# Four 128-column turns a head, from TensorE to VectorE blocks and two transfers, in a decoder step with a gated delta rule

## The chip, the cores and the metric

The kernel runs on one core of one Trainium2 chip. The metric is the device time of one execution in microseconds (us), from its first to its last instruction with what the chip adds around it; a time is given as the median of several runs. A profile is one further execution, recorded instruction by instruction; its span is the time between the first and the last recorded instruction.

The engines are named as in the profile: PE is TensorE (PEld its weight loads), DVE is VectorE, ACT is ScalarE, POOL is GpSimd, and SP is SyncE, which here only issues DMAs. Each engine works through its own list in order. An engine that waits for something holds up everything behind it in its list.

## The reference

One inference step of a one-layer decoder: 512 prompt tokens and 8 sample tokens, model width 2048, in float32. The first half of the layer mixes tokens by two groups, a gated delta network of 8 heads of dimension 128 and a multi-scale pool; the second half is a gated feed-forward network of width 5632. What the change touches is the delta network of the prompt. Cut to that, with `c` a chunk of tokens:

```python
q, k = l2norm(q) * HEAD_DIM ** -0.5, l2norm(k)          # per head, over its 128 channels
gc = cumsum(g); decay = tril(exp(gc[:, None] - gc[None, :]))
m = strict_tril((k * beta) @ k.T * decay)               # (I + m) is inverted
u = solve(I + m, v * beta); w = solve(I + m, k * beta * exp(gc))
qk = tril(q @ k.T * decay)
for each chunk:                                         # S is the 128 x 128 state
    v_new = u - w @ S
    o = (q * exp(gc)) @ S + qk @ v_new
    S = S * exp(g_last) + (k * exp(g_last - gc)).T @ v_new
dn_out = rmsnorm(o, dn_norm) * silu(z)
```

`q`, `k`, `v` come from one input projection, a causal convolution over 4 tokens and silu. `dn_out` and the pool's output go through an output projection, are added to the input, and the feed-forward part follows.

## The kernel before, in words

Nearly all of the work is matrix products in three passes: each operand is cut into a high and a low float32r part (ScalarE copies the high part, VectorE subtracts for the low one), and high x high, high x low and low x high are summed (L168 to L170 in the first half, L1222 to L1224 in the second). Weights stream in as pieces of 512 KB ("raw", three buffers), issued by SyncE (L131); ScalarE (L135) and VectorE (L137) cut each piece, with a priority ahead of all other work.

The first half runs over tiles of 128 output columns: `product` does 16 steps of 6 passes into two accumulators of 264 and 256 columns. The order of the tiles is: keys of heads 0 to 3, the output gate z of heads 0 to 3, queries and values of heads 0 to 3, the same for heads 4 to 7, then the pool's tiles. The first two key tiles belong to the start of the kernel. Activations are held with channels on the 128 partitions and tokens along them; `qkv_tile` (L730) makes the convolution and silu of one tile in this form.

The small work of the delta network is woven in between the steps of the products. A `Weave` (L43) holds tasks that are Python generators: after each step of a product it lets a task go on to its next `yield n`, which asks to be called again n steps later. TensorE's order is exactly the order in which the program is written. The other engines' orders in this part are made by a planner that takes an instruction when its inputs are expected and follows the priorities. In the second half all orders are as written.

The tasks, with 128 tokens (a chunk) at a time, four chunks to a head:

- `gates` makes the decay exponents once, and writes them to DRAM (`gcr_d`, L621).
- `keys(h)` (L760): `decay(h)` (L743) fetches the head's decay row for all partitions (`gcb`) and makes the decay matrix `dm`; the product of the keys with themselves goes to `gp_` (L766); the keys are turned to tokens on partitions by four TensorE transposes (L769) into `ktp`. ScalarE sums squares of `ktp`, GpSimd takes the root (`pow_mhalf`, L215: `rr`), VectorE scales `gp_` to `nn` (L781) and the turned keys to `kd` (L783). Four DMAs (L788) then store the 32x32 diagonal blocks of `nn` in DRAM (`nd_d`), and GpSimd zeroes them (L791).
- `eliminate(b)` (L794), for four heads at once: the blocks come back as `nb` (L797), 31 steps of two VectorE operations (L807, L809) invert them into `u`, and the inverse and its transpose go to DRAM (`ud_d`, L810, L813).
- `qv_tiles(h)` (L1089) fetches the inverse into `utf` by four DMAs (L1093), makes the query tile, then the value tile, and adds `delta`.
- `delta(h)` (L817) makes the decay again; multiplies `nn` with the inverse (L831); turns the queries (L838) for the sums of their squares and the root `fq`; refines the inverse in three steps (`for it`, L846: products L850, correction L852 into `cur`, named `uu` in the trace), with the query-key product (L857) and `aq` (L860) in step 0 and the turn of the values (L865) and their scaling to `vs` (L867) in step 1. Then the recurrence runs over the four chunks: `R` (L879), `W` (L884, L886), the state `S` (L889, L894) and the output in `op_` (L895, L896). At the end the output is normed into `on`, in the place of `nn`.
- `gate(h)` (L913) turns `on` back by four transposes (L916) and multiplies it into the silu of z (L918).

The transposes write to PSUM, so ScalarE and VectorE read the turned form there.

Of the kernel before, what the change touches and what calls it, by code (L numbers as in the profile page):

```python
# [17 lines left out]
P = 128  # L18
D = 2048
KT = D // P  # L20
NB = 8
SEQ = 512
NTOK = NB + SEQ
H = 8
# [12 lines left out]
    "qts": 1, "fq": 2, "aq": 1, "vs": 1, "R": 2, "W": 2, "S": 2, "so": 2, "ro": 2, "s0": 2, "s2": 1, "kd": 4, "st": 2,  # L37
# [32 lines left out]
def decoder_kernel(ctx, tc, x_prompt, x_sample, state_delta, state_conv, state_pool, norm_mix, w_in,  # L70
# [450 lines left out]
    with ExitStack() as p1:  # L521
# [29 lines left out]
        def gates():  # L551
# [69 lines left out]
            sp.dma_start(gcr_d, gr)  # L621
# [120 lines left out]

        def decay(h):  # L743
# [16 lines left out]
        def keys(h):  # L760
            kT, nn = mixb[:, h % 4, 0:SEQ], mixb[:, 4 + h % 4, 0:SEQ]
            kd = kds[h] = d1tile("kd", [P, SEQ], "kd")
# [4 lines left out]
            ktp = pst()  # L767
            for c in range(NCH):
                te.transpose(ktp[:, ck(c)], kT[:, ck(c)], ident)  # L769
            ss = d1tile("ss", [P, NCH], "ss")  # L770
            squares(ktp, ss)
# [11 lines left out]
            dve.tensor_tensor(v3(kd), v3(ktp), bc3(ad), op=ALU.mult)  # L783
            yield 6 if h < 3 else 2
            nn3 = v3(nn)
            for q in range(4):
                r = slice(32 * q, 32 * q + 32)
                sp.dma_start(nd_d[h, q].rearrange("c s j -> s c j"), nn3[r, :, r])  # L788
# [5 lines left out]
        def eliminate(b):  # L794
            hs = slice(4 * b, 4 * b + 4)
            nb = d1tile("nb", [64, 32, 32], "nb")
            sp.dma_start(nb.rearrange("p s j -> p (s j)"), nd_d[hs].rearrange("h q c s j -> (h q c) (s j)"))  # L797
# [12 lines left out]
            sp.dma_start(ud_d[hs, :, 0].rearrange("h q c s j -> (h q) c (s j)"), uf)  # L810
            ut = d1tile("nb", [64, 32, 32], "ut")
            dve.tensor_copy(ut, u.rearrange("p s j -> p j s"))
            sp.dma_start(ud_d[hs, :, 1].rearrange("h q c s j -> (h q) c (s j)"), ut.rearrange("p s j -> p (s j)"))  # L813
# [3 lines left out]
        def delta(h, qT, vT):  # L817
# [18 lines left out]
            qtp = pst()  # L836
            for c in range(NCH):
                te.transpose(qtp[:, ck(c)], qT[:, ck(c)], ident)  # L838
            ss = d1tile("ss", [P, NCH], "ss")
            squares(qtp, ss)  # L840
            dve.tensor_scalar(ss, ss, EPS, None, op0=ALU.add)
            fq = d1tile("fq", [P, NCH], "fq")
            pow_mhalf(fq, ss)
            dve.tensor_scalar(fq, fq, float(P) ** -0.5, None, op0=ALU.mult)
            yield 2
            for it in range(3):  # L846
# [7 lines left out]
                if it == 0:  # L854
                    gq_ = pst()
# [6 lines left out]
                if it == 1:  # L862
                    vtp = pst()
                    for c in range(NCH):
                        te.transpose(vtp[:, ck(c)], vT[:, ck(c)], ident)  # L865
                    vs = d1tile("vs", [P, SEQ], "vs")
                    dve.tensor_tensor(v3(vs), v3(vtp), bc3(ik), op=ALU.mult)  # L867
# [4 lines left out]
            for c in range(NCH):  # L872
                if S is None:
                    R = vs[:, ck(c)]
                else:
# [3 lines left out]
                    dve.scalar_tensor_tensor(Rt, kp[:, 0:P], negc[:, c, h:h + 1], vs[:, ck(c)],  # L879
                                             op0=ALU.mult, op1=ALU.add)  # L880
# [17 lines left out]
                yield 1  # L898
            sp.dma_start(nd_prompt[0, 0, h], S)
# [11 lines left out]
            weave.add(gate(h, on), 1, 8)  # L911

        def gate(h, on):  # L913
            otp = pst()
            for c in range(NCH):
                te.transpose(otp[:, ck(c)], on[:, ck(c)], ident)  # L916
            yield 1
            dve.scalar_tensor_tensor(mix[h][:, NB:NTOK], otp, dnw, mix[h][:, NB:NTOK], op0=ALU.mult, op1=ALU.mult)  # L918
# [170 lines left out]
        def qv_tiles(h):  # L1089
            utf = utfs[h % 2].rearrange("p a c j -> p (a c) j")  # L1090
            for q in range(4):
                r = slice(32 * q, 32 * q + 32)
                sp.dma_start(utf[r, :, r], ud_d[h, q].rearrange("a c s j -> s (a c) j"))  # L1093
            qT = d1tile("s0", [P, SEQ], "qT")
            qkv_tile(0, h, qT)
            vT = d1tile("s2", [P, SEQ], "vT")
            qkv_tile(2, h, vT)
            weave.add(delta(h, qT, vT), 0, 1)

        kds = {}  # L1100
        for b in range(2):
            for h in range(4 * b, 4 * b + 4):
                qkv_tile(1, h, mixb[:, h % 4, 0:SEQ],
                         {0: ext_first, 1: ext_second}.get(h))
                if h == 0:
                    weave.add(states())
                    weave.add(gates(), 1)
# [969 lines left out]
```

## Time and profile before

| | us |
|---|---|
| runs | 2160.15, 2160.83, 2162.0 |
| median of the runs | 2160.83 |
| profiled execution: span | 2158.9 |
| PE busy | 2136.1 (99%) |
| DVE busy | 1746.4 (81%) |
| ACT busy | 929.6 (43%) |
| POOL busy | 433.8 (20%) |
| granted TensorE clock | 0.999 |

Of the profiled execution the span is all that is recorded; the runs' times have a little more around it. The first half of the layer lasts until about 615 us, and the work that the change touches lies between about 75 and 520 us.

How to read the rows: an instruction is named by its line in the kernel, its engine, its operation, and the tiles out<-in by the program's names. "x8" counts instructions. In groups, the two numbers behind the shapes are busy us and mean ns of one; what follows is the idle time of the engine just before them and what ended it. In a view of waits, "A <- B: 2.4, 3, 1.1" says that A waited for B for 2.4 us in total, 3 times, at most 1.1 us. In a timeline the first column is the start in us, the second the duration of the (merged) row. TensorE's instructions overlap in its pipeline, so the distance between two starts, not the duration, is what one costs.

### The profile page before, as it was taken

How to read it: one execution, taken by the hardware profiler on the slowest of the kernel's cores; microseconds unless marked ns; L12 is line 12 of the kernel's file. 1: busy time of each engine (PE TensorE's matmuls, PEld its weight loads, DVE VectorE, ACT ScalarE, POOL GpSimd, SP SyncE). 2: the span in 40 equal slices, each digit the busy share in tenths (PEclk: the TensorE clock that was granted, in tenths of full speed). 3: DMA queues.
4: the chain of work that ended last, by engine and by line, in shares of the span. 5: the costliest groups of instructions: out<-in, count | busy, mean ns of one | idle time of the engine just before them, and what ended most of it. 6: DMA issues, size and time to landing. Idle time of an engine off the chain costs nothing.

```text
span 2158.9 us, 42980 instructions
## 1 busy us (share of the span) xinstructions
PE 2136.1 (99%) x17809; PEld 2128.8 (99%) x17809; DVE 1746.4 (81%) x2619; ACT 929.6 (43%) x1404; POOL 433.8 (20%) x512
## 2 busy tenths in 40 slices
PE   8999999999999999999999999999999999999998
PEld 7999999999999999999999999999999999999998
DVE  7786667666499979988988888888877898887997
ACT  6533443432264545434433434434334444435444
POOL 2210110111012202233233233232113302003100
PEclk9999999999999999999999999999999999999999
DMA  8343234323445543554554454454446746438343
GB/s 281 92 110 91 76 94 112 88 76 96 120 121 161 152 119 111 155 166 141 145 166 139 147 167 143 142 163 134 125 147 189 234 111 205 115 103 247 93 108 119
DMA packets 442497, 297.04 MB, mean 138 GB/s; under 512 B 26556, under 2 KB 423253, under 8 KB 438957
## 3 DMA queue, kind: packets, MB, share of 16 engines
q1 hardware_dynamic: 422733, 219.94, 36.3%
q0 software_dynamic: 18256, 73.55, 10.5%
q8 instruction: 139, 2.28, 0.5%
q10 hardware_dynamic: 1312, 0.80, 0.1%
q14 instruction: 57, 0.47, 0.1%
HBM read 251.47 MB, written 43.43 MB: 137 GB/s over the span
## 4 chain that ended last, share of the span: by engine, by line
PE 86%; DVE 8%; DMA 2%; issue 2%; ACT 1%; POOL 1%; SPq 0%; DVEq 0%; POOLq 0%; ACTq 0%
PE dn L1223 20%; PE dn L1222 20%; PE dn L1224 20%; PE mm L168 6%; PE mm L170 6%; PE mm L169 6%; DVE lo L1216 2%; DVE raw L1244 1%; PE dn L850 1%; DMA st<-a_d 1%; DVE lo L137 1%; POOL st L1776 0%; DMA xt<-in_x_prompt_dram 0%; PE dn L960 0%; PE dn L857 0%
## 5 line engine op out<-in xcount | busy, mean ns | idle before, releaser
L1215 ACT CAST hi<-raw 128x1024 fp32r<-128x1024 f32 (+1 forms) x422 | 427.4, 1027 | 400.2 <-DVE raw L1244 206.5
L1216 DVE TENSOR_TENSOR lo<-raw,hi 128x1024 fp32r<-128x1024 f32 (+1 forms) x422 | 527.4, 1270 | 87.1 <-ACT hi L1215 85.6
L168 PE MATMUL mm<-xh,hi 128*128 128x256 f32 (+1 forms) x1280 | 379.7, 297 | 2.4 <-DVE mixa L259 2.4
L169 PE MATMUL mm<-xl,hi 128*128 128x256 f32 (+1 forms) x1280 | 361.5, 282 | 0.9 <-DVE xl L350 0.7
L170 PE MATMUL mm<-xh,lo 128*128 128x256 f32 (+1 forms) x1280 | 361.8, 283 | 0.4 <-DVE lo L137 0.4
L168 PEld LDWEIGHTS mm<-xh,hi 128*128 128x128 f32 x1280 | 241.4, 189 | 3.7 <-DVE mixa L259 3.1
L169 PEld LDWEIGHTS mm<-xl,hi 128*128 128x128 f32 x1280 | 241.7, 189 | 1.7 <-DVE xl L350 1.7
L170 PEld LDWEIGHTS mm<-xh,lo 128*128 128x128 f32 x1280 | 240.8, 188 | 0.6 <-DVE lo L137 0.6
L1244 DVE TENSOR_TENSOR raw<-raw 128x1024 f32<-128x1024 f32 (+1 forms) x130 | 175.3, 1349 | 2.2
L1223 PE MATMUL dn<-b21l,hi 128*128 128x260 f32 x620 | 175.7, 283 | 0.4 <-DVE b21l L1786 0.4
L1224 PE MATMUL dn<-b21h,lo 128*128 128x260 f32 x620 | 175.4, 283 | 0.0
L1222 PE MATMUL dn<-b21h,hi 128*128 128x260 f32 x620 | 175.0, 282 | 0.0
L1224 PE MATMUL dn<-b11h,lo 128*128 128x260 f32 x612 | 173.4, 283 | 1.2 <-DVE lo L1216 1.1
L1223 PE MATMUL dn<-b11l,hi 128*128 128x260 f32 x612 | 173.3, 283 | 0.0
L1222 PE MATMUL dn<-b11h,hi 128*128 128x260 f32 x612 | 172.7, 282 | 0.0
L1222 PE MATMUL dn<-T1h,hi 128*128 128x260 f32 x556 | 158.1, 284 | 0.0
L1223 PE MATMUL dn<-T1l,hi 128*128 128x260 f32 x556 | 157.7, 284 | 0.0
L1224 PE MATMUL dn<-T1h,lo 128*128 128x260 f32 x556 | 156.7, 282 | 0.0
L1222 PE MATMUL dn<-B22h,hi 128*128 128x260 f32 x548 | 155.9, 284 | 0.0
L1223 PE MATMUL dn<-B22l,hi 128*128 128x260 f32 x548 | 155.6, 284 | 0.0
L1224 PE MATMUL dn<-B22h,lo 128*128 128x260 f32 x548 | 154.6, 282 | 0.4 <-DVE lo L1216 0.4
L135 ACT CAST hi<-raw 128x1024 fp32r<-128x1024 f32 (+2 forms) x86 | 87.1, 1014 | 148.2 <-PE mm L169 139.4
(659 smaller groups left out, 6422.5 us busy)
## 6 DMA issues: line engine op xcount, KB each, us to landing
raw<-in_w_gate_up_dram SPq DMA_DIRECT2D x134, 512.0 KB
raw<-in_w_in_dram SPq DMA_DIRECT2D x79, 512.0 KB
a_d<-mixa POOLq DMA_DIRECT2D x22, 1040.0 KB, 5.5
raw<-in_w_down_dram SPq DMA_DIRECT2D x48, 448.0 KB
mixb<-in_w_gate_up_dram SPq DMA_DIRECT2D x41, 512.0 KB
raw<-in_w_out_dram SPq DMA_DIRECT2D x25, 512.0 KB
st<-a_d POOLq DMA_DIRECT2D x49, 260.0 KB, 6.5
raw<-in_w_down_dram SPq DMA_DIRECT2D x24, 512.0 KB
```

The lines of the kernel that those rows point to most:

```text
L135: act.copy(hi[:, r], raw[:, r])
L137: dve.tensor_tensor(lo[:, r], raw[:, r], hi[:, r].bitcast(F32), op=ALU.subtract)
L168: te.matmul(acc[ci], wh, hi[k][:, c0:c1], start=(k == 0), stop=False)
L169: te.matmul(acc[ci], wh, lo[k][:, c0:c1], start=False, stop=False)
L170: te.matmul(acc[ci], wl, hi[k][:, c0:c1], start=False, stop=(k == len(w) - 1))
L850: te.matmul(yp[0:96, c, j], xt_[:, c, :], udf[:, c, j] if it == 0 else v3(cur)[:, c, j], start=True, stop=True)
L1215: act.copy(hi, raw)
L1216: dve.tensor_tensor(lo, raw, hi.bitcast(F32), op=ALU.subtract)
L1222: te.matmul(acc, wh[:, k, :], xf[:, k, :], start=start and k == 0, stop=False)
L1223: te.matmul(acc, wh[:, k, :], xg[:, k, :], start=False, stop=False)
L1224: te.matmul(acc, wl[:, k, :], xf[:, k, :], start=False, stop=stop and k == wh.shape[1] - 1)
L1244: dve.tensor_tensor(r[name], r[a], r[b], op=op)
```

## The change

Each of the four turns of a head leaves TensorE. `turn_blocks(kind, h, src, dst)` lets VectorE transpose the 32x32 blocks of a 128x512 tile in place in their grid (`bt`), SyncE writes the result to a DRAM tile `tok_d`, and four more DMAs read it back in another order, so that the blocks change places as well. Kinds 1 (keys) and 3 (normed output) are read in pieces of 128 bytes; for kinds 0 (queries) and 2 (values) VectorE writes the blocks so that the pieces have 512 bytes, and the turned tile has its columns in another order, which the views `by_chunk` and `by_column` undo.

With that, the order of several steps changes. The key tile is turned as soon as it is made, into `kd`, and scaled later, in step 0 of the refinement. The squared norms of the keys are the diagonal of `gp_`, read by VectorE with the unit matrix. The value tile is made and turned before the query tile. The query-key product and `aq` go from step 0 to step 2 of the refinement. The turned queries are only used for their norms, by ScalarE after the second chunk. The output is turned at the end of `delta`, and `gate` comes 12 steps later instead of 8.

The DMAs of the decay rows (`gcr_d`, `gcb`), of the diagonal blocks (`nd_d`, `nb`) and of the inverse (`ud_d`, `utf`) are issued by GpSimd instead of SyncE. The descriptor scratch is 8192 instead of its default, and the tiles `vs`, `bt` and `tq` get 2, 2 and 1 buffers of 128x512.

```diff
-            sp.dma_start(gcr_d, gr)
+            pool.dma_start(gcr_d, gr)
...
+        tok_d = dram.tile([4, H, P, SEQ], F32, name="tok_d")
+        def by_chunk(a):
+            return a.rearrange("p (i c q) -> p c i q", i=4, c=NCH)
+        def by_column(a):
+            return a.rearrange("p (i q) -> p i q", i=4)
...
+        def turn_blocks(kind, h, src, dst):
+            bt, d = d1tile("bt", [P, SEQ], "bt"), tok_d[kind, h]
+            if kind % 2:
+                dve.transpose(bt, src)
+                d = d.rearrange("p f -> (p f)").rearrange("(c p f) -> c p f", c=NCH, p=P)
+                sp.dma_start(d.rearrange("c p f -> p c f"), v3(bt))
+                rows = d.rearrange("c (i p) (j q) -> j p (c i) q", p=32, q=32)
+            else:
+                dve.transpose(bt.rearrange("p (j c q) -> p c j q", j=4, c=NCH),
+                              src.rearrange("p (c j q) -> p c j q", j=4, c=NCH))
+                sp.dma_start(d, bt)
+                rows = d.rearrange("(i p) (j f) -> j p i f", p=32, j=4)
+            for j in range(4):
+                sp.dma_start(dst[32 * j:32 * j + 32, :].rearrange("p (n q) -> p n q", n=rows.shape[2]), rows[j])
...
-            sp.dma_start(gcb, gcr_d[h:h + 1, :].broadcast_to([P, SEQ]))
+            pool.dma_start(gcb, gcr_d[h:h + 1, :].broadcast_to([P, SEQ]))
...
-            ktp = pst()
+            ss = d1tile("ss", [P, NCH], "ss")
+            junk = d1tile("junk", [P, P], "junk")
             for c in range(NCH):
-                te.transpose(ktp[:, ck(c)], kT[:, ck(c)], ident)
-            ss = d1tile("ss", [P, NCH], "ss")
-            squares(ktp, ss)
+                dve.scalar_tensor_tensor(junk, gp_[:, ck(c)], 1.0, ident, op0=ALU.mult, op1=ALU.mult,
+                                         accum_out=ss[:, c:c + 1])
...
-            dve.tensor_tensor(v3(kd), v3(ktp), bc3(ad), op=ALU.mult)
...
-                sp.dma_start(nd_d[h, q].rearrange("c s j -> s c j"), nn3[r, :, r])
+                pool.dma_start(nd_d[h, q].rearrange("c s j -> s c j"), nn3[r, :, r])
...
-            qtp = pst()
-            for c in range(NCH):
-                te.transpose(qtp[:, ck(c)], qT[:, ck(c)], ident)
...
                 if it == 0:
+                    dve.tensor_tensor(v3(kd), v3(kd), bc3(sck[:, h, 2, :]), op=ALU.mult)
+                if it == 2:
                     gq_ = pst()
...
                 if it == 1:
-                    vtp = pst()
-                    for c in range(NCH):
-                        te.transpose(vtp[:, ck(c)], vT[:, ck(c)], ident)
-                    vs = d1tile("vs", [P, SEQ], "vs")
-                    dve.tensor_tensor(v3(vs), v3(vtp), bc3(ik), op=ALU.mult)
+                    scaled(vs, ik)
...
-            weave.add(gate(h, on), 1, 8)
+            turn_blocks(3, h, on, on)
+            weave.add(gate(h, on), 1, 12)
         def gate(h, on):
-            otp = pst()
-            for c in range(NCH):
-                te.transpose(otp[:, ck(c)], on[:, ck(c)], ident)
+            dve.scalar_tensor_tensor(mix[h][:, NB:NTOK], on, dnw, mix[h][:, NB:NTOK], op0=ALU.mult, op1=ALU.mult)
             yield 1
...
-                sp.dma_start(utf[r, :, r], ud_d[h, q].rearrange("a c s j -> s (a c) j"))
+                pool.dma_start(utf[r, :, r], ud_d[h, q].rearrange("a c s j -> s (a c) j"))
+            vs = d1tile("vs", [P, SEQ], "vs")
+            qkv_tile(2, h, vs)
+            turn_blocks(2, h, vs, vs)
             qT = d1tile("s0", [P, SEQ], "qT")
             qkv_tile(0, h, qT)
-            vT = d1tile("s2", [P, SEQ], "vT")
-            qkv_tile(2, h, vT)
-            weave.add(delta(h, qT, vT), 0, 1)
+            qk = d1tile("tq", [P, SEQ], "qk")
+            turn_blocks(0, h, qT, qk)
+            weave.add(delta(h, qT, qk, vs), 0, 1)
...
+                kds[h] = d1tile("kd", [P, SEQ], "kd")
+                turn_blocks(1, h, mixb[:, h % 4, 0:SEQ], kds[h])
                 weave.add(keys(h), 1, 16)
...
-    nc = _bacc.Bacc("TRN2", target_bir_lowering=False, num_devices=1)
+    nc = _bacc.Bacc("TRN2", target_bir_lowering=False, num_devices=1, dynamic_dma_scratch_size=8192)
```

More of the change, by code (lines that the diff above doesn't have):

```diff
@@ L873, in delta @@
                 if S is None:
[L874 removed]
+                    R = by_chunk(vs)[:, c]
                 else:
@@ L898, in delta @@
                 yield 1
+                if c == 1:
+                    ss = d1tile("ss", [P, NCH], "ss")
+                    junk = d1tile("junk", [P, P], "junk")
+                    for j in range(NCH):
+                        act.activation(by_column(junk), by_chunk(qk)[:, j], AF.Square, accum_out=ss[:, j:j + 1])
+                    dve.tensor_scalar(ss, ss, EPS, None, op0=ALU.add)
+                    fq = d1tile("fq", [P, NCH], "fq")
+                    pow_mhalf(fq, ss)
+                    dve.tensor_scalar(fq, fq, float(P) ** -0.5, None, op0=ALU.mult)
             sp.dma_start(nd_prompt[0, 0, h], S)
```

26 lines of the change are left out of this document (11 added, 15 removed).

## The prediction, made before the result was known

> **What bounds the kernel now.** I read the page first, for its span and the busy time of the engines.
>
> ```profile
> span 2158.9 us, 42980 instructions
> PE 2136.1 (99%) x17809; PEld 2128.8 (99%) x17809; DVE 1746.4 (81%) x2619; ACT 929.6 (43%) x1404; POOL 433.8 (20%) x512
> ```
>
> TensorE is idle for 22.8 us of 2158.9. Whatever leaves its list shortens the run, unless a wait takes its place. This span is 1.9 us below the median of the runs, 2160.83; I sum against the span and add 1.9 at the end. About 0.2%, 4.3 us, is what a measurement of this kernel can tell from no change.
>
> Next the stretches view, for the stages that the change touches. The columns are the stretch, its length, then busy time and instructions of PE, PEld, DVE, ACT and POOL, the granted clock, the share of the DMA engines and GB/s.
>
> ```profile
> 84.00:112.00 28.00, 28.00 (x239) 28.00 (x238) 21.34 (x70) 17.86 (x45) 7.09 (x18) 1.00 0.39 108
> 112.00:118.00 6.00, 5.08 (x43) 4.87 (x42) 2.48 (x5) 4.10 (x6) 0.79 (x4) 1.00 0.67 187
> 118.00:150.00 32.00, 30.48 (x252) 30.06 (x251) 29.81 (x77) 7.77 (x10) 0.46 (x1) 1.00 0.36 98
> 150.00:180.00 30.00, 30.00 (x263) 30.00 (x261) 20.12 (x40) 11.68 (x21) 4.44 (x10) 1.00 0.45 112
> 180.00:300.00 120.00, 120.00 (x1041) 120.00 (x1040) 75.84 (x178) 52.51 (x120) 12.58 (x29) 1.00 0.30 81
> ```
>
> These are the key work of heads 0 to 3 (84 to 112), their elimination (118 to 150, VectorE 93% busy) and their recurrences (from 150, VectorE 63 to 67%). TensorE stands still only between 112 and 150, by 0.92 + 1.52 us. The view of waits names the cause:
>
> ```profile
> PE mm L168 <- DVE mixa L259: 2.4, 3, 1.1
> ```
>
> It is an eviction of a z product that stands in VectorE's list between steps of the elimination. Everything else that the turns feed comes in time today. So the account has two sides: TensorE time removed, and cover lost on VectorE, GpSimd and the queues.
>
> **What is removed.** Four groups of four transposes a head, 32 groups: keys (L769), queries (L838), values (L865), gated output (L916). The instruction view counts them, with duration min/median/max in ns:
>
> ```profile
> L769 PE MATMUL dn<-ident,mixb x32: 272/273/273, 83.0 to 328.4; 128*128 128x128 f32 x32
> L838 PE MATMUL dn<-ident,qT x32: 272/272/273, 162.8 to 485.1; 128*128 128x128 f32 x32
> L865 PE MATMUL dn<-ident,vT x32: 272/273/281, 168.3 to 491.3; 128*128 128x128 f32 x32
> L916 PE MATMUL dn<-ident,mixb x32: 270/272/273, 198.0 to 518.3; 128*128 128x128 f32 x32
> ```
>
> Those durations overlap in the pipeline, so 128 x 272 ns would be far too much. The price is the distance between starts, in the timeline:
>
> ```profile
> 162.76 0.60 PE L838 MATMUL dn<-ident,qT 128*128 128x128 f32 x4
> 163.12 0.37 PE L168 MATMUL mm<-xh,hi 128*128 128x264 f32 x1
> 163.32 0.28 PE L169 MATMUL mm<-xl,hi 128*128 128x264 f32 x1
> 163.44 0.28 PE L170 MATMUL mm<-xh,lo 128*128 128x264 f32 x1
> ```
>
> The product goes on 0.36 us after the group begins. Its first pass then takes 0.20 us instead of 0.12; that 0.08 goes too only where nothing else of that kind stands in the same place. So a group is worth 0.36 to 0.44 us, 32 groups 11.5 to 14.1; I take 0.40, **-12.8 us**. No matrix product is added, and the query-key product (L857) only moves two steps later.
>
> The Trainium skill ("VectorE: DVE Perf Modes", sections on the three transpose paths and rules for kernel authors) speaks against this: a 128x128 transpose belongs on TensorE where PSUM will do as its target, as VectorE turns only 32x32 blocks. By that rule the groups would be worth their place, and the change would end at the first rival below or worse. The rows above speak against it here: the engine that it would use is the one without idle time.
>
> **What is added on VectorE.** Its prices, from the groups and the instruction view (mean ns, or min/median/max):
>
> ```profile
> L825 DVE TENSOR_TENSOR qts<-qT,gcb 128x512 f32<-128x512 f32 x8 | 5.5, 687 | 1.4 <-ACT qT L740 1.4
> L737 DVE TENSOR_SCALAR y<-ext,prm 128x512 f32<-128x512 f32 x24 | 12.9, 536 | 0.5
> L812 DVE COPY ut<-u x2: 1117/1122/1128, 146.5 to 369.6; 64x1024 f32<-64x1024 f32 x2
> L781 DVE SCALAR_TENSOR_TENSOR mixb<-dn,sck,dm 128x128 f32<-128x128 f32 x32 | 9.0, 342 | 0.0
> ```
>
> No block transpose is in this trace. Its nearest rows, all of 128x512, give 0.54 (one input) to 0.69 us; the strided copy, 1024 elements in 1.12, gives 0.56 for 512. I take 0.65, with 1.12 as the upper end. Four a head are 2.6 us. The key norms, now read off the diagonal of the key product, cost 4 x 0.34 = 1.4 us and free ScalarE of its squares. The scaling of the keys (one more operation of 128x512, 0.69) moves from the key work into the recurrence. So VectorE gets 4.0 us a head more, 32 us in all, in stages where it idles about a third of the time. That costs nothing by itself; the price is in three places where the cover is thin.
>
> *First, heads 0 to 3.* Between 84 and 112 VectorE has 6.7 us left; four heads bring 4 x (0.65 + 1.4 - 0.69) = 5.4. It fits only if nothing waits, so I put the start of the elimination 2 to 6 us later, and it then runs at VectorE's own speed. Its end leads to the first matrix product of the recurrence:
>
> ```profile
> 147.63 0.54 SPq L813 DMA_DIRECT2D ud_d<-ut  x1
> 150.75 1.32 SPq L1093 DMA_DIRECT2D utf<-ud_d  x3
> 153.55 2.55 SPq L1093 DMA_DIRECT2D utf<-ud_d  x5
> 157.91 0.62 POOL L835 COPY uu<-utf 128x512 f32<-128x512 f32 x1 [3.54 <-DMA utf<-ud_d]
> 161.90 1.03 PE L831 MATMUL dn<-utf,mixb 128*128 128x96 f32 x8
> ```
>
> The inverse lands at 157.9, TensorE asks at 161.9: 4.0 us of cover. Four key groups less bring TensorE there 1.6 us earlier, 2.4 left. On SyncE's list the fourth piece went out at 153.55, 1.48 after the first three, because a weight load stood between; on GpSimd's list it need not, which gives back 1.5. Against 3.9 of cover a delay of 2 to 6 us is a wait of 0 to 2.1; with evictions held up as between 112 and 150 now, I take **+2.0** (bounds 0 and 6). Heads 4 to 7 have a key product between their key work, and I charge them nothing.
>
> *Second, the refinement steps.* The correction of the inverse has this cover:
>
> ```profile
> 164.64 0.84 PE L850 MATMUL dn<-utf,xt__2137 128*96 128x96 f32 x8
> 166.89 0.55 DVE L852 SCALAR_TENSOR_TENSOR uu<-dn,utf 96x384 f32<-96x384 f32 x1
> 167.69 0.81 PE L850 MATMUL dn<-uu,xt__2137 128*96 128x64 f32 x8
> 172.81 0.27 ACT L886 COPY W<-dn 128x128 f32<-128x128 f32 x1
> 174.04 0.38 PE L889 MATMUL dn<-W,kd 128*128 128x128 f32 x2
> ```
>
> From the first eight products to the next are 3.05 us. The eight of L857 that fill part of it (some 0.8 at 0.09 to 0.11 each, a quarter of a group) leave this place, so 2.25 remain, and the correction needs 0.84 for its products, 0.55 for itself and about 0.1 between. That leaves 0.7 with VectorE free; the scaling of the keys or a block transpose (0.65 to 0.69) just ahead of it uses this up. The ScalarE copy at 172.81 ends 0.96 before its reader, and the query squares now come near it. The scores of L857 are made nearer to their reader as well. For all of these I charge 0.35 us a head, **+2.8 us** (bounds 0 and 10, the latter 1.25 a head).
>
> *Third, GpSimd's list and VectorE behind it.* 87 DMAs come onto it: 16 decay rows and their source, 32 diagonal blocks, 6 around the elimination, 32 of the inverse. Issue and landing there, from later stages, and VectorE's waits for GpSimd's roots:
>
> ```profile
> L1421 POOL DMA_DIRECT2D ub<-u_d x16: 550/550/550, 848.5 to 1451.0; - x16
> L1429 POOL DMA_DIRECT2D out_dram<-ub x16: 803/803/803, 861.8 to 1463.9; - x16
> DMA to landing us min/median/max: 2.8/3.1/4.6
> DVE fq L844 <- POOL fq L215: 9.1, 8, 1.1
> ```
>
> 87 x 0.55 to 0.80 is 48 to 70 us on a list that is busy for a quarter of these stages at most. It fits. Behind each DMA stand the memsets of the diagonal blocks, the copies of the inverse and the roots, three a head, and VectorE waits for a root with its whole list (1.1 us now). A root behind one issue costs VectorE 0.8 more, which its idle third bears. I charge nothing beyond the above; the bounds are 0 and the slower rival. The smaller descriptor scratch (8192) has no row that it changes; I charge nothing.
>
> **What is added on SyncE.** 160 turn DMAs come, the 87 go: 73 more. Each write must land before its four reads are issued, and the weight loads stand in the same list:
>
> ```profile
> L788 SPq DMA_DIRECT2D nd_d<-mixb x32: 303/428/435, 91.3 to 335.0; - x32
> q1 hardware_dynamic: 80337, 39.70, 34.1%
> SPq L131 <- DVE lo L137: 205.7, 48, 18.5
> ACT hi L135 <- PE mm L169: 90.9, 34, 5.6
> ```
>
> From the queue's row (84 to 520 us) a packet takes 0.341 x 436 x 16 / 80337 = 29.6 ns on average. A key or output turn is 512 packets out and 2048 back, a query or value turn 128 and 512: 6400 a head, 51200 in all, 95 us of 16 engines if a 128-byte packet takes what the mean one does. The share would rise from 0.34 to 0.56. A turn holds SyncE for about 3 us (147.63 to 150.75 above, write to first read) and 4 x 0.43, some 5 us; three of them in the two products of a head, 2 x 96 passes of 0.12 or 23 us, leave room for the loads. Loads wait today for buffers, up to 18.5 us, and the cuts for TensorE. With three buffers of half a product each a load goes out 3 x 5.8 = 17 us ahead of its cut, so 5 us more behind a turn are borne. The values are turned one product (11.5 us) ahead of their use, and the queries only for their norms, which no matrix product reads. The output turn has no TensorE behind it. Price **0**.
>
> **The sum.** -12.8 + 2.0 + 2.8 = -8.0, so 2150.9 for the span and **2152.8 us** for the runs.
>
> **The rivals.** *Cover used up, no change.* Lost cover costs what the transposes gave: a VectorE operation of 0.65 stands ahead of each correction and the key scaling ahead of another, 1.25 us a head, 10 us, and 2 for heads 0 to 3. -12.8 + 12 = -0.8: 2160.0. For it: the correction ended at 167.44, 0.25 before its reader, though it could have ended 1.3 earlier; VectorE's order, not its load, sets this. Against: one such row only, and VectorE waited for a root (L844) just there, which now stands elsewhere.
>
> *GpSimd's list holds VectorE: slower.* GpSimd takes its list in order. If a DMA that waits for a landing (2.8 to 4.6 us), or for an eviction, stands ahead of a root or of the inverse, VectorE stops at the root, and the correction, evictions and state updates stand behind it. With 24 roots each 3.1 later and 2 of those reaching TensorE, 48 us: 2160.83 - 12.8 + 48 = 2196; with half of the roots 2172. It decides from 17.1 us of new waits (12.8 + 4.3), 0.7 a root. For it: nd_d's waits are on this list. Against: POOL is idle nine tenths of the recurrence. The Trainium skill ("SBUF — State Buffer", section on two separate sides) states a rule with the same effect: GpSimd cannot write descriptors while VectorE holds the shared port in a two-port mode. This trace shows such a lock once, the other way round, the second row beside a GpSimd memset:
>
> ```profile
> 160.75 0.50 DVE L737 TENSOR_SCALAR y<-ext,prm 128x512 f32<-128x512 f32 x1
> 149.51 1.27 DVE L737 TENSOR_SCALAR y<-ext,prm 128x512 f32<-128x512 f32 x1
> ```
>
> 0.77 us lost once. The page's case goes from about 620 to 3100 ns an issue; four pieces of the inverse would then come 10 us later, an estimate from that page by which this rival would win.
>
> *The change doesn't do what it says:* TensorE waits where each group stood, because the group covered a wait; the time stays at 2160.8, and its chance is part of that of no change. Against: TensorE has no idle time from 150 to 300, so nothing was late with the groups there, and only the refinement step above has less cover than a group takes.
>
> **How the numbers follow.** The forecast has 0.64, with a range of its own from 2146.7 (nothing but 14.1 saved) to 2156.5. No change has 0.20, the slower rival 0.14, and 0.02 goes to a gain beyond 14.1 because the waits of 112 to 150 shrink. Faster is 0.64 + 0.02 = 0.66, the same 0.20, slower 0.14. The range for 8 in 10 is 2146 to 2164: below are 0.03, above most of the slower rival's 0.14 and the edge of no change.
>
> **What would show it.** Right: 128 TensorE instructions fewer, no idle time of TensorE beyond 1 us a head between 150 and 520, the first L831 or its successor at about 160 to 163, the stage's end near 8 us earlier and all later stages as long as now. A wait of TensorE for the inverse shows the first place, one for the correction (uu) the second, one of VectorE for a root longer than 1.5 us the third. Wrong would be weight cuts that wait for loads, TensorE waiting for values (vs) or keys (kd), or a block transpose above 1.2 us.

## The result, and the profile after

The changed kernel takes 2175.7 us (median of 4 runs, 2174.51 to 2176.0) where the kernel before took 2161.19 beside it: a ratio of 1.0066, 95% interval 1.0054 to 1.0079. It is slower by 14.5 us; 8.0 us less had been forecast, in a range that ended at 2164.

From here on a few lines of the kernel have new numbers: L859 is the product with the inverse (L831 before), L869 and L871 the refinement's product and correction, L779 `dm`, L776 the decay row, L816 the diagonal blocks, L825 `nb`, L835 and L837 the elimination's steps, L984 the product with the sample states, L805 the scales made from a root, L810 `nn` (`mixb` in the trace), L819 the memsets, L894 and L909 a product with the state and the state's copy. In the kernels of the experiments a line can lie a few numbers off. The page of the changed kernel first:

```profile
span 2172.6 us, 43049 instructions
...
PE 2131.2 (98%) x17681; PEld 2122.2 (98%) x17681; DVE 1772.8 (82%) x2715; ACT 920.9 (42%) x1340; POOL 482.6 (22%) x599
```

TensorE has exactly 128 instructions less and is idle for 41.4 us instead of 22.8. The view of waits, TensorE alone, says where:

```profile
PE mm L168 <- DVE mixa L259: 5.8, 3, 5.1
PE dn L859 <- DMA utf<-ud_d: 5.5, 1, 5.5
...
PE dn L984 <- DMA s<-in_state_delta_dram: 3.8, 1, 3.8
PE dn L869 <- DVE uu L871: 2.8, 6, 0.5
...
PE dn L894 <- DVE S L909: 2.0, 1, 2.0
```

These five causes make 19.9 us; of them only evictions of z cost anything before (2.4). So 17.5 us of waits are new: a z eviction at 110, the inverse at 166, a state update at 281, the sample states at 536, and six short ones for the correction.

The stretches view has the columns of the prediction; the eighth figure, the granted clock, was 1.00 in all five rows of before. The first five rows are the stages quoted there, the others the stretches behind the four long waits:

```profile
84.00:112.00 28.00, 26.50 (x223) 26.29 (x221) 21.36 (x87) 12.46 (x16) 14.13 (x30) 1.00 0.55 129
112.00:118.00 6.00, 2.41 (x11) 2.41 (x12) 4.74 (x17) 2.89 (x4) 3.76 (x9) 0.64 0.53 139
118.00:150.00 32.00, 31.43 (x250) 31.02 (x250) 23.15 (x57) 10.47 (x14) 2.69 (x8) 0.96 0.39 101
150.00:180.00 30.00, 24.23 (x192) 23.88 (x191) 21.13 (x45) 5.97 (x7) 12.88 (x22) 0.89 0.50 126
180.00:300.00 120.00, 116.44 (x988) 115.71 (x987) 79.03 (x179) 51.28 (x120) 15.81 (x33) 0.99 0.47 121
```

```profile
116.00:123.00 7.00, 7.00 (x43) 7.00 (x43) 3.43 (x9) 3.79 (x5) 4.08 (x10) 0.68 0.50 117
172.00:179.00 7.00, 7.00 (x52) 7.00 (x52) 4.06 (x7) 2.29 (x3) 3.62 (x6) 0.77 0.24 56
284.00:288.00 4.00, 4.00 (x23) 4.00 (x23) 2.27 (x7) 1.92 (x4) 0.72 (x2) 0.57 0.89 209
540.00:544.00 4.00, 4.00 (x21) 4.00 (x22) 0.00 (x0) 0.48 (x1) 0.00 (x0) 0.57 0.00 1
```

Behind each long wait TensorE is busy without a gap, but at a clock of 0.57 to 0.77. That loses 7 x 0.32 + 7 x 0.23 + 2 x 4 x 0.43 = 7.3 us more. With the removal at 0.36 a group (11.5 us, the lower bound given) the account is 17.5 + 7.3 - 11.5 = +13.3; the spans differ by 13.7.

What is late ahead of the first wait is seen in the timeline of VectorE, then of GpSimd (start, duration, engine, line; in brackets the wait of the engine and its releaser):

```profile
100.70 0.35 DVE L779 SCALAR_TENSOR_TENSOR dm<-gcb,gcs,mneg 128x128 f32<-128x128 f32 x1 [1.39 <-DMA gcb<-gcr_d]
...
107.56 0.16 DVE L805 TENSOR_TENSOR sck<-rr 128x4 f32<-128x4 f32 x1 [1.31 <-POOL rr L215]
...
115.11 0.42 DVE L259 TENSOR_TENSOR mixa<-mm,rb 128x264 f32<-128x264 f32 x1
115.45 0.86 DVE L810 SCALAR_TENSOR_TENSOR mixb<-dn,sck,dm 128x128 f32<-128x128 f32 x3
...
126.88 0.20 DVE L835 TENSOR_TENSOR tm<-nb,u 64x31 f32<-64x31 f32 x1 [7.45 <-DMA nb<-nd_d]
```

```profile
116.61 2.24 POOL L816 DMA_DIRECT2D nd_d<-mixb  x4 [1.76 <-DVE mixb L810]
118.84 0.58 POOL L776 DMA_DIRECT2D gcb<-gcr_d  x1
119.45 0.95 POOL L819 MEMSET mixb<- 32x128 f32 x4
120.36 0.54 POOL L825 DMA_DIRECT2D nb<-nd_d  x1
```

The z eviction at 115.11, for which TensorE stood since 110.2, has its place in VectorE's list behind key work that came late. The elimination starts at 126.88, after four block issues, a row, four memsets and a read in GpSimd's list, and a landing. Before:

```profile
109.80 1.12 DVE L781 SCALAR_TENSOR_TENSOR mixb<-dn,sck,dm 128x128 f32<-128x128 f32 x4
...
118.64 0.20 DVE L807 TENSOR_TENSOR tm<-nb,u 64x31 f32<-64x31 f32 x1 [0.30 <-DMA nb<-nd_d]
```

So the start is 8.2 us later. Of this, 5.4 lie ahead of the end of the last `nn` (116.31, before 110.92), 0.5 between there and the issue of the read (120.36, before 114.47), and 2.4 in the read itself (6.5 us from issue to use, before 4.2). From 82 us to that `nn` VectorE waited about as long as before: 3.2 us for rows, 4.5 for roots and 0.8 for TensorE, against 2.2, 4.2 and 1.6. So nearly all of the 5.4 is work that was added to it. The start orders the experiments.

### The profile page after: what moved, and what is told of

Same layout as the page of the kernel before. It is cut to its first block, busy times and chain, and to the rows that moved or that the text cites. A ratio compares the mean times of both kernels' runs of the same rounds, so it can differ in the third digit from the quotient of the medians.

```text
span 2172.6 us, 43049 instructions
## 1 busy us (share of the span) xinstructions
PE 2131.2 (98%) x17681; PEld 2122.2 (98%) x17681; DVE 1772.8 (82%) x2715; ACT 920.9 (42%) x1340; POOL 482.6 (22%) x599
## 4 chain that ended last, share of the span: by engine, by line
PE 73%; DVE 6%; DMA 2%; issue 1%; ACT 1%; POOL 1%; DVEq 0%; SPq 0%; POOLq 0%; ACTq 0%
PE dn L1252 21%; PE dn L1251 21%; PE dn L1253 21%; PE mm L168 3%; PE mm L169 2%; PE mm L170 2%; DVE lo L1245 1%; DMA st<-a_d 1%; DVE raw L1273 1%; DVE lo L137 0%; POOL st L1805 0%; DMA vs<-tok_d 0%; PE dn L984 0%; DVE u L837 0%; DVE tm L835 0%
## 5 line engine op out<-in xcount | busy, mean ns | idle before, releaser
L1437 POOL TENSOR_TENSOR mixa<-mixa 128x520 f32<-128x520 f32 x22 | 51.0, 2319 | 494.7 <-DVE mixa L1431 494.7
```

What stands on the lines that cost most here:

```text
L1437: pool.tensor_tensor(q[:, 4:8:2, :], q[:, 1:4:2, :], q[:, 0:2, :], op=ALU.subtract)
```

## The experiments

Each kernel was timed beside the kernel before on the same chip (that one's medians were 2160.91 to 2161.59). "Start" is the first elimination's first step.

| kernel | median us | ratio, 95% interval | start |
|---|---|---|---|
| before | 2161.19 | | 118.6 |
| after | 2175.70 | 1.0054 to 1.0079 | 126.9 |
| 1 keys on TensorE | 2174.31 | 1.0044 to 1.0074 | 125.4 |
| 2 all DMAs on SyncE | 2188.61 | 1.0110 to 1.0140 | 138.9 |
| 3 lists only | 2173.40 | 1.0039 to 1.0073 | 126.5 |
| 4 key turn only | 2170.82 | 1.0026 to 1.0056 | 127.2 |
| 5 decay rows only | 2166.03 | 1.0013 to 1.0032 | 123.9 |
| 6 blocks only | 2166.75 | 1.0017 to 1.0037 | 123.7 |
| 7 inverse only | 2161.45 | 0.9991 to 1.0011 | 118.5 |
| 8 turns without keys | 2162.54 | 0.9997 to 1.0016 | 118.6 |
| 9 states on GpSimd | 2156.46 | 0.9969 to 0.9987 | 118.4 |
| 10 scores early | 2175.99 | 1.0054 to 1.0079 | 118.4 |
| 11 key turn, lists on SyncE | 2191.68 | 1.0124 to 1.0152 | 140.7 |
| 12 key turn late | 2155.32 | 0.9961 to 0.9984 | 119.7 |

Two theories stood at the start. A: VectorE's added key work (block transpose, norms) makes heads 0 to 3 late. B: GpSimd's list does.

**1. Keys on TensorE.** The changed kernel with the key turns, norms and scaling of before.

```diff
-                turn_blocks(1, h, mixb[:, h % 4, 0:SEQ], kds[h])
+                te.transpose(ktp[:, ck(c)], kT[:, ck(c)], ident)
```

> The changed kernel with the key turns back on TensorE, as before the change (transposes, squares by ScalarE, scaling in the key work); the other three turns and GpSimd's list stay. Theory A (the key work of heads 0 to 3 is what came late: an eviction at 110 us and the inverse at 166 us, 10.9 us of TensorE's waits and 4.4 us of half clock behind them): 2175.7 + 3.2 for eight groups of transposes - 15.3 = 2163.6. Theory B (the DMAs on GpSimd's list made them late): no less than 2175.7, near 2179.

2174.31, 1.4 less than the changed kernel (and than the least that B allowed), and the elimination starts 1.5 earlier. A falls as the sole cause: without VectorE's own key work only 1.5 of the 8.2 us go. The reason is that the two overlap: VectorE now waits 7.4 us for rows in the key work instead of 3.2.

**2. All DMAs on SyncE.** The changed kernel with its 87 DMAs back on SyncE.

```diff
-            pool.dma_start(gcb, gcr_d[h:h + 1, :].broadcast_to([P, SEQ]))
+            sp.dma_start(gcb, gcr_d[h:h + 1, :].broadcast_to([P, SEQ]))
```

(and six more lines like it)

> The changed kernel with the 87 DMAs of decay rows, diagonal blocks and inverse back on SyncE; the four turns stay. Theory A (key work on VectorE): the waits at 110 and 166 us stay, the one at 281 us (decay row on GpSimd's list) may go: 2172 to 2176. Theory B (GpSimd's list): the waits at 110, 166 and 281 us and their half clock go, 19.2 us: about 2156.5.

Neither: 2188.61, the wait for the inverse grew to 23 us (waits view):

```profile
PE dn L859 <- DMA utf<-ud_d: 23.1, 1, 23.1
```

So B is not the whole either: with the turns on SyncE, that list is the worse place.

**3. Lists only.** The kernel before with the 87 DMAs on GpSimd and the small scratch, and nothing else.

> The kernel before with only the 87 DMAs moved to GpSimd's list and the smaller descriptor scratch; all turns on TensorE. Theory A (key work on VectorE): within 2 us of the kernel before. Theory B (GpSimd's list): slower by at least 8 us, up to 19.

B holds: +11.8 us without a single turn. What is seen in the timelines of GpSimd and VectorE:

```profile
92.57 2.25 POOL L788 DMA_DIRECT2D nd_d<-mixb  x4 [1.18 <-DVE mixb L781]
94.81 0.57 POOL L746 DMA_DIRECT2D gcb<-gcr_d  x1
```

```profile
99.33 0.35 DVE L749 SCALAR_TENSOR_TENSOR dm<-gcb,gcs,mneg 128x128 f32<-128x128 f32 x1 [4.25 <-DMA gcb<-gcr_d]
...
133.59 0.42 DVE L259 TENSOR_TENSOR mixa<-mm,rb 128x264 f32<-128x264 f32 x1
```

A decay row is issued behind the four blocks of an earlier head, which wait for VectorE's `nn`; VectorE then stops 4.25 us for the row, with the z evictions behind it in its list (TensorE waits 3.2 us). The largest wait of TensorE, 5.3 us, is for the z eviction at 133.59, which stands between the steps of an elimination that started 7.8 late. Before, this row too stood behind four blocks, in SyncE's list, and went out 1.7 us earlier, at 93.12. So the place behind the blocks is not new; VectorE's list is another one as well: before, it had the norms and scales of the earlier head ahead of this `dm`, here it has them behind.

**4. Key turn only.** The changed kernel with queries, values and output turned on TensorE again (as before at L838, L865, L916).

> The changed kernel with only the key turn by VectorE and transfers; queries, values and output are turned on TensorE as before, and GpSimd's list stays. Theory A (key work on VectorE): the kernel before - 3.2 + 15.3, near 2173, with TensorE waiting near 110 and 165 us. A third theory, C (SyncE's list with 160 turn DMAs and the values' turn inside the elimination): the eviction wait may stay but the inverse comes in time: 2161 to 2166.

2170.82: 4.9 less than the changed kernel, 2.2 under A's number and above C's range, so neither as stated. The wait for the sample states is gone and one of the six for the correction is left (0.5 us), so these belong to the turns of queries, values and output, or to the steps that move with them (the query-key product is back in step 0 here). The inverse still comes 2.3 us late.

The question was now what in GpSimd's list costs: its order (O) or a later landing of its DMAs (T). Experiments 5 to 7 split experiment 3 into its parts; each is the kernel before with the named DMAs on GpSimd and the small scratch.

```diff
# 5
-            sp.dma_start(gcr_d, gr)
+            pool.dma_start(gcr_d, gr)
...
-            sp.dma_start(gcb, gcr_d[h:h + 1, :].broadcast_to([P, SEQ]))
+            pool.dma_start(gcb, gcr_d[h:h + 1, :].broadcast_to([P, SEQ]))
# 6: nd_d and nb in the same way; 7: ud_d and utf
```

**5. Decay rows only.**

> The kernel before with only the decay rows (their source and 16 rows, 17 DMAs) on GpSimd's list, scratch 8192; the other 70 moves and all transposes as before. With all 87 moves there, 11.8 us were lost without any turn. Theory O (order in the list): a row is late because it stands behind the four diagonal blocks of the head before (issued at 94.81 behind them, VectorE stopped 4.25 us for it). Without the blocks on that list the row goes out in time: 2160 to 2163.5, no eviction wait above 1.5 us. Theory T (transfer): every move issued by GpSimd lands later (3.4 to 4.4 us), and the parts of the list add up: rows alone 2164.5 to 2167.

**6. Blocks only.**

> The kernel before with only the 32 diagonal blocks and the 2 reads of them ahead of the elimination (34 DMAs) on GpSimd's list, scratch 8192. Theory O: the rows go out on SyncE in time, so the key work keeps its pace; what is left is the chain from the last block to the start of the elimination (7.8 us before, 11.7 with the whole list), 2 to 4 us on evictions there: 2162 to 2166. Theory T: blocks bring the larger share of the 11.8 us, 2166.5 to 2170.

**7. Inverse only.**

> The kernel before with only the inverse (its two writes a group of four heads and 32 reads, 36 DMAs) on GpSimd's list, scratch 8192. From the end of the elimination to the first use of the inverse there were 11.4 us on SyncE's list and 10.8 on GpSimd's, so both theories expect no loss: 2159.5 to 2162.5, no wait of TensorE for the inverse. Above 2165 the inverse's own list would be a cost that neither has.

The medians are 5.1, 5.8 and 0.5 above the kernel before; the sum, 11.4, is the 11.8 of experiment 3. These are T's numbers. But the trace does not show T's cause for the rows. On SyncE a row issued at 98.03 was used at 101.96, after 3.9 us; on GpSimd in experiment 5 one issued at 93.51 was used at 97.15, after 3.6. What is late is the issue. The row that SyncE issued at 103.13 (first row, before) goes out at 107.76 on GpSimd (experiment 5: GpSimd's timeline, then SyncE's):

```profile
103.13 0.34 SPq L746 DMA_DIRECT2D gcb<-gcr_d  x1
```

```profile
106.64 0.20 POOL L791 MEMSET mixb<- 32x128 f32 x1 [0.23 <-DMA nd_d<-mixb]
107.76 0.60 POOL L746 DMA_DIRECT2D gcb<-gcr_d  x1 [0.92 <-DVE mixb L781]
...
120.09 0.20 POOL L791 MEMSET mixb<- 32x128 f32 x1 [1.61 <-DMA nd_d<-mixb]
```

```profile
115.10 0.58 SPq L788 DMA_DIRECT2D nd_d<-mixb  x1
```

It is not the memsets ahead of it that hold this row, though they wait for the blocks to land: they were done at 106.84, and the row went on waiting for VectorE's `nn`. VectorE's stops grew little, for rows from 2.2 to 2.9 us and for roots from 4.2 to 5.0, and its last `nn` came some 2 us late (it starts at 112.13, before at 109.80). The read of the blocks went out 5.7 late, at 120.17: the last block was issued at 115.10, behind a weight load at 114.66, where before the weight load came behind all the blocks, and the memset behind it waited until 120.09. That order on SyncE is a cost that neither O nor T names.

In experiment 6 memsets that wait for blocks stand ahead of a root, and VectorE stops for the root, and later for the blocks:

```profile
103.60 0.70 POOL L791 MEMSET mixb<- 32x128 f32 x3 [1.72 <-DMA nd_d<-mixb]
104.77 0.20 POOL L791 MEMSET mixb<- 32x128 f32 x1 [0.47 <-DMA nd_d<-mixb]
105.05 1.04 POOL L215 TENSOR_TENSOR rr<-ss,mhalf 128x4 f32<-128x4 f32 x1
```

```profile
106.13 0.16 DVE L776 TENSOR_TENSOR sck<-rr 128x4 f32<-128x4 f32 x1 [2.75 <-POOL rr L215]
...
123.74 0.20 DVE L807 TENSOR_TENSOR tm<-nb,u 64x31 f32<-64x31 f32 x1 [5.74 <-DMA nb<-nd_d]
```

So O was wrong in that it needed rows and blocks together: either part costs nearly half by itself. For the read `nb` the landing is slower too: issued at 119.08 and used at 123.74, 4.7 us, where SyncE's took 4.2 (114.47 to 118.64). In all the traces these reads took 4.4 to 6.5 us from GpSimd and 3.5 to 5.0 from SyncE. As each of GpSimd's went out 0.5 to 1.7 us behind a weight load, neither the issuing engine nor the load is shown to be the cause, and how much of the 5.8 this is stays open.

**8. Turns without keys.** Experiment 1 with rows and blocks back on SyncE; the inverse stays on GpSimd.

> The changed kernel with the key turns back on TensorE and the decay rows and diagonal blocks back on SyncE; queries, values and outputs turn by blocks through SyncE, the inverse stays on GpSimd's list. Theory O: the key work and the elimination keep the pace of the kernel before; 24 groups of 0.40 leave TensorE (-9.6), the correction's waits stay (+2.8), the sample states' wait at about 535 stays with the half clock behind it (+5.5): 2158 to 2163. Rival S (SyncE's list): the turns' writes, which wait for VectorE, hold the weight loads, rows and inverse behind them as where all moves stood on SyncE (2188.6): 2168 or more.

2162.54, inside the first theory's range: the first stage keeps its pace, and the gain of the turns goes into two other waits:

```profile
PE dn L983 <- DMA s<-in_state_delta_dram: 3.4, 1, 3.4
PE dn L870 <- DVE uu L872: 2.9, 6, 0.5
```

**9. States on GpSimd.** Experiment 8 with the sample states' reads on GpSimd.

```diff
-                sp.dma_start(s0, state_delta[0, 4 * hf:4 * hf + 4, h].rearrange("b k v -> k b v"))
+                pool.dma_start(s0, state_delta[0, 4 * hf:4 * hf + 4, h].rearrange("b k v -> k b v"))
```

> As turns without keys (2162.5), with the 16 reads of the sample states issued by GpSimd instead of SyncE. There TensorE waited 3.4 us for them at 522 (3.7 from start to start), and the half clock behind that took 3.4 us at 0.5, so 1.7 more. If the read was late because SyncE's list held it behind a weight load and an output turn, both go: 2157 to 2158.5, the six waits for the correction stay. If the read is late because its buffer is freed late, it waits on GpSimd as well: 2161 to 2163.

2156.46, a little under the range, and that wait is gone: the read had stood in SyncE's list, not for its buffer. This kernel beats both. Its account: 24 groups x 0.36 = 8.6, less 2.9 for the correction, is 5.7; measured are 4.7.

**10. Scores early.** Experiment 9 with the query-key product back in step 0 of the refinement.

```diff
-                if it == 2:
+                if it == 0:
                     gq_ = pst()
```

> As states on GpSimd, with the query-key product put back from the third refinement step into the first. Theory: the correction stands behind the convolution's pieces in VectorE's list (three of 0.74 ahead of it), and the product's 0.9 us between the two groups of eight cover that; the six waits (2.9 us in all) go: 2.5 to 3 us below states on GpSimd, 2154 to 2156. Rival: the four score operations (1.1 us) then stand in VectorE's list ahead of other readers and the wait comes back at the next step: within 1 us of states on GpSimd.

Neither: 2175.99. The waits for the correction are gone, but this took their place:

```profile
PE dn L877 <- ACT qT L740: 15.3, 8, 3.0
```

The change makes the query tile last, so in step 0 the queries are not there yet. TensorE now waits between the two groups of the correction, so this run does not show whether the product would have covered it. The move of this product to step 2 is no choice; it follows from turning the values first.

**11. Key turn, lists on SyncE.** The changed kernel with rows and blocks back on SyncE, the inverse on GpSimd.

> The changed kernel with only the decay rows and diagonal blocks back on SyncE; all four turns by blocks, the inverse on GpSimd's list. It differs from turns without keys (2162.5) by the key turn alone. Theory (two lists, each too late): on SyncE the rows and blocks stand behind the key turn's reads and the weight loads, as where all moves were there (elimination started at 138.9 against 118.6, TensorE waited 23.1 for the inverse); the inverse itself no longer stands behind a turn's write, which gives back some 10 us: 2172 to 2180. Rival: the rows and blocks were late on GpSimd only, and the key turn pays its eight groups: 2158 to 2162.

The theory was right in its sign and too small: 2191.68. The inverse on GpSimd gave nothing back against experiment 2, so it had not stood behind a turn; it was late because the elimination was (start at 140.7). SyncE's list shows why:

```profile
86.06 0.47 SPq L621 DMA_DIRECT2D gcr_d<-gr  x1
86.63 2.13 SPq L771 DMA_DIRECT2D kd<-tok_d  x4
95.86 0.39 SPq L131 DMA_DIRECT2D raw<-in_w_in_dram  x1
96.29 0.58 SPq L776 DMA_DIRECT2D gcb<-gcr_d  x1
```

The first decay row goes out at 96.29, behind the reads of a key turn and a weight load that waits for its buffer; before, it went out at 82.27.

**12. Key turn late.** Experiment 9 with the key turn again by blocks, but placed behind the elimination.

```diff
         def qv_tiles(h):
...
+            kds[h] = d1tile("kd", [P, SEQ], "kd")
+            turn_blocks(1, h, mixb[:, h % 4, 0:SEQ], kds[h])
             vs = d1tile("vs", [P, SEQ], "vs")
```

> As states on GpSimd (2156.5), with the key turn back on blocks, but placed behind the elimination, ahead of each head's value product, where the keys are first needed; norms from the diagonal and scaling in the first refinement step as in the changed kernel. Theory: what made the key turn dear was its place in SyncE's list ahead of the rows and blocks; placed late it gives its 8 groups of 0.36 (2.9 us), against 0.7 us a head more on VectorE ahead of the elimination (1.4 for the norms, 0.7 less for the scaling), which starts up to 2.9 later than at 118.4 and holds two evictions by 1 to 3 us in all: 2153.5 to 2157. Rival: the transpose and the scaling stand ahead of corrections in VectorE's list and the write and reads ahead of the values' in SyncE's: more waits for uu or vs, 2158 to 2166.

2155.32, within its range, the start only 1.3 later than in experiment 9. In its profile the waits for the correction rose from 2.9 to 4.8 us, as the rival said, without the rival's time. The intervals of 9 and 12 overlap, so the key turn's own gain isn't shown; that its place made it dear is, against experiment 11: of the 36.4 us between them the sample states, which are also moved here, account for the 6.1 between experiments 8 and 9.

## Why the prediction was wrong, point by point

- **What is removed, -12.8.** Right at its lower bound, or a little under it: with 11.5 the account of the spans closes within 0.4, and experiment 9 got 4.7 us out of 24 groups after 2.9 of waits, which is 0.32 a group.
- **GpSimd's list, 0: the step that failed.** Measured alone, +11.8 (experiment 3). "It fits" compared the issue times with GpSimd's idle time. The issues cost what was said (the rows' took 0.58, the inverse's 0.58 to 0.66); what the move does to the order was not priced. A row goes out behind four block issues (2.24 us) that wait for `nn`, a root stands behind memsets that wait for blocks (experiment 6), and VectorE stops for both. But the order in GpSimd's list is not all that the move changes. At 281 a state update stands behind a `dm` that waits for its row (VectorE's timeline, after, then experiment 8):

```profile
280.61 0.35 DVE L779 SCALAR_TENSOR_TENSOR dm<-gcb,gcs,mneg 128x128 f32<-128x128 f32 x1 [2.72 <-DMA gcb<-gcr_d]
280.88 0.75 DVE L941 SCALAR_TENSOR_TENSOR mixa<-mixb,prm,mixa 128x512 f32<-128x512 f32 x1
...
282.68 0.28 DVE L909 COPY S<-dn 128x128 f32<-128x128 f32 x1
```

```profile
266.30 0.74 DVE L940 SCALAR_TENSOR_TENSOR mixa<-mixb,prm,mixa 128x512 f32<-128x512 f32 x1
...
268.58 0.29 DVE L908 COPY S<-dn 128x128 f32<-128x128 f32 x1 [0.41 <-PE dn L905]
268.79 0.60 DVE L779 SCALAR_TENSOR_TENSOR dm<-gcb,gcs,mneg 128x128 f32<-128x128 f32 x2
```

That row was not late in GpSimd's list. It went out at 276.63, 0.3 us behind the `dm` that freed its buffer, and was used 4.0 later; SyncE's in experiment 8 went out at 264.86 and was used 3.9 later. What differs is VectorE's list: from SyncE the gate's product of an output, a weight cut and the copy of the state come ahead of this `dm`, from GpSimd they come behind it. Experiments 1 and 8, which differ in the rows and blocks alone, have these same two orders, with a stop of 2.2 us in experiment 1 and none in 8. So the planner orders VectorE otherwise when another engine issues the row. How the 11.8 divide between that order, GpSimd's own and the landings stays open; that the move as a whole costs them is shown.

- **Heads 0 to 3, +2.0, bounds 0 and 6.** The start came 8.2 later, of which 7.8 come with the lists alone and 1.5 go with the key turn (they overlap). The elimination also lasted longer, 32.6 us (to 159.43) instead of 27.8, with two more weight cuts and the first evictions and convolutions of the next product between its steps. Only the way over the inverse was priced. The shorter way is the z eviction that stands behind key work in VectorE's list: 5.1 us at 110, and 5.5 for the inverse at 166. Of the evictions' and the inverse's waits 8.9 us are new, beyond the bound of 6. That VectorE's scaling of the keys "moves into the recurrence" was wrong for these heads: the planner put it among the key work (95.9 to 117.6).
- **Heads 4 to 7, nothing.** No eviction waited there in the changed kernel, but the wait at 281 (2.0 us, and the half clock behind it) hangs on a `dm` of these heads' keys; experiments 1, 3 and 4 also show an eviction that waits (1.6 to 2.6 us, at 362 to 365).
- **The refinement steps, +2.8.** Right in its number: six waits, 2.8 us, for a correction that stands behind VectorE's other work. The work is not what was named, though. No block transpose and no scaling of the keys stands just ahead, but three pieces of the convolution and the scaling of the values; experiment 1, where the keys are scaled elsewhere, has the same waits (2.9). That the number fits to the tenth is luck. (VectorE, after:)

```profile
206.47 2.32 DVE L739 SCALAR_TENSOR_TENSOR y<-ext,prm,y 128x512 f32<-128x512 f32 x3
208.71 0.55 DVE L871 SCALAR_TENSOR_TENSOR uu<-dn,utf 96x384 f32<-96x384 f32 x1
```

- **SyncE's list, 0.** Wrong by 3.8 us and the clock behind it: no weight load was late, but the sample states' read was; it had not been looked for in that list. Moved in experiment 9, it gave 6.1. The turned values came late once, too (VectorE waited 4.0 us for them at 172), but beside TensorE's wait for the inverse.
- **The clock.** Not in the prediction at all, 7.3 us.
- **The slower rival** named the list and its point, 17.1 us of new waits; there were 17.5, and the time lies in its range of 2172 to 2196. That it does is in part luck: by its own sum 17.5 us of waits give 2165.5, and the half clock, which it did not have, adds 7.3. Its price by late roots was not what happened: VectorE's waits for the roots were as long as before (9.0 and 9.1 us after, 8.1 and 9.1 before), while those for rows and blocks rose from 2.2 and 1.6 to 5.9 and 8.9. The rule of the Trainium skill ("SBUF — State Buffer", section on two separate sides) that was weighed there is that a DMA issued by GpSimd grows from some 620 to 3100 ns when VectorE holds the shared port. It is not seen in this trace: no issue of the moved DMAs took over 0.96 us.

Some of the evidence for the right answer was in the trace of before: z evictions waited 2.4 us there already, the only waits of this part, and VectorE stood 2.25 for a row at 101.96 with the row on SyncE. A stage whose cover is used up has no free step.

## What to carry to other kernels

Price a DMA that moves to another engine's list by its neighbours there: what it waits for, what then waits behind it, and which engine stops for that; the engine's idle share says nothing. Where a planner orders the engines, look at the other engines' lists again after the move, for they can change with it (experiment 8 against 1). In a stage where the bottleneck already waits a little, expect a delay to be lost. A turn through DRAM was cheap where nothing else on its queue was urgent, which can be a matter of placing it some steps later (experiment 12 against 11).

## What the runs showed of the hardware

TensorE's granted clock falls to half after a wait, also in the middle of a run. Of the gaps between two starts of TensorE in all fourteen kernels, from 80 us on, all 14 of 3.7 us or more had a stretch at 0.5 in them or right behind them, of the 19 between 1.9 and 3.6 twelve, of 50 between 0.9 and 1.8 none. A stretch can begin inside a long wait. But for the one at the end of each run, the stretches last 3.4 us or a multiple: 6.8, and 23.9, most of it inside waits of 23 and 25 us. The Trainium skill ("TensorE: Matmul & The Clock Gate", section on the HAM clock gate) gives a free-running window of 3413 ns, and the lengths agree with it. The same page (section on why this matters for your kernels) asks for no idle gaps above some 3 us; gaps of 1.9 and 2.0 us (experiments 12 and 1) halved the clock here, so that limit is too generous for this kernel.

A VectorE block transpose of 128x512 took 0.70 us, the diagonal norm 0.28 (lines view, after):

```profile
L761 DVE STREAM_TRANSPOSE bt<-mixb 128x512 f32<-128x512 f32 x16 | 11.3, 704 | 0.9 <-ACT mixb L740 0.9
L799 DVE SCALAR_TENSOR_TENSOR junk<-dn,ident 128x128 f32<-128x128 f32 x32 | 9.1, 284 | 1.5 <-PE dn L795 1.3
```
